# A decoder step on one core: the sampled tokens' attention handed out in 27 small steps between the prompt's steps, in place of nine large ones

## The chip, the cores and the metric

The kernel runs on one core of a Trainium2 chip. The metric is the device time of one launch in microseconds (us). A core has five engines that run their own instruction queues in order: TensorE (PE in the profile, with its weight loads as PEld), VectorE (DVE), ScalarE (ACT), GpSimd (POOL) and SyncE (SP), which here only issues DMA transfers.

## The reference, cut to what matters

One decoder layer. 1024 prompt tokens and 8 x 8 sampled tokens (8 sequences, 8 new tokens each) go through the same weights. Each token's normalised input is projected to three head groups: a gated short convolution, a dilated sliding-window attention of 6 heads (B), and a sliding-window attention with sinks of 6 query and 2 key heads (C). Their outputs go through one output projection; then comes a second norm and a SwiGLU feed-forward network.

```python
def apply_layer(x, mod, mixer, g_mix, g_ffn, w_out, w_gate_up, w_down):
    shift1, scale1, gate1, shift2, scale2, gate2 = mod
    mix, states = mixer(rmsnorm(x, g_mix) * (1 + scale1) + shift1)
    x = x + gate1 * (mix @ w_out)
    x = x + gate2 * swiglu(rmsnorm(x, g_ffn) * (1 + scale2) + shift2, w_gate_up, w_down)
```

The sampled tokens attend over a cache of past keys and values in HBM (2048 positions for B, 128 for C, for each of 8 sequences) and over their own 8 new tokens: scores, a masked softmax, and the weighted sum of values. The prompt tokens need nothing of the cache.

## The kernel before, in words

Activations lie transposed, 128 channels by 1088 tokens. The tokens are cut into three column groups, 0 to 365, 366 to 731 (both prompt only) and 732 to 1087, whose last 64 columns are the sampled tokens. A product in full precision is done as three matmuls per block of 128 rows (`mm3`, L204 to L206: high by high, high by low, low by high); a weight half (256 KB) is loaded by SP (`load`, L97, five buffers `wraw`) and split into a high and a low part on ScalarE (L90) and VectorE (L91; four buffers `wsp`).

After the prompt's attention two things are open: the sampled tokens' attention, and, for the first two column groups, everything that follows. Two generators hold them:

- `sample_steps` first does the three C head pairs, each with 2 x 128 cached positions, then the three B head pairs (p = 0, 1, 2). For a B pair: key loads of 512 KB (`stream_in`, L658 and L660, seven buffers `raw`), scores on TensorE (`scores`, L667) in three segments of 512, 512 and 264 columns, a running minimum on VectorE after each (`mins`, L671; scores are negated), then in `probs` one exponential over the whole row (L680), transposes (L690) and their copies (L691), then in `weigh` the products with the values (L701) for the two halves `par` of the sequences, each over 10 value blocks and the new tokens (`vn`), a scaled copy (L704), two transposes (L707) and copies into `mixS` (L712). Each B pair loads 10 key and 10 value tiles.
- `ahead_steps` holds the first two column groups' further way, 24 steps: two that split the attention output (`split_mix`), eight of the output projection (`w_out`, 48 matmuls each, with L768 to add the result), one for the root mean squares (`rstd`: squares L798, sums L799, L802; root L233 to L239, with the square root on ScalarE at L234; broadcast L806), one for the second norm (`second_norm`: L823 on VectorE, L825 on ScalarE, L826 on VectorE, eight blocks for each column group), four of gate and up (`gate_up`, 96 matmuls each, followed by a modulation tile, `late_mod`, whose loads `wmod` use the same `wraw` buffers and whose products are L179), and eight of the down projection (24 matmuls each).

The loop before gives two steps of `ahead_steps` after every step of `sample_steps`; the rest follows. Then the third column group, which holds the sampled tokens, is split into `mx` (L619 to L624), which needs all of `mixS`, and goes through the output projection.

The code's order is not the last word: the framework that builds the kernel puts each engine's instructions into an order by a timeline of its own, within what the data and the buffers allow. The queues on the chip are then fixed.

## Time and profile before

| what | value |
|---|---|
| median of 3 runs | 1393.7 us (1387.84 to 1393.89) |
| the profiled execution's own time | 1396.23 us |
| its span | 1394.2 us |
| TensorE busy | 1345.8 us (97%) |
| VectorE, ScalarE, GpSimd busy | 850.7, 596.0, 199.1 us |
| DMA | 190.90 MB, mean 137 GB/s |

The profile is of one execution. Its busy time of TensorE counts overlapping matmuls as busy, so the places where the engine stands are read from the timelines, not from the share. Times in the rows are us from the start of the span.

### The profile page before, as it was taken

How to read it: one execution, taken by the hardware profiler on the slowest of the kernel's cores; microseconds unless marked ns; L12 is line 12 of the kernel's file. 1: busy time of each engine (PE TensorE's matmuls, PEld its weight loads, DVE VectorE, ACT ScalarE, POOL GpSimd, SP SyncE). 2: the span in 40 equal slices, each digit the busy share in tenths (PEclk: the TensorE clock that was granted, in tenths of full speed). 3: DMA queues.
4: the chain of work that ended last, by engine and by line, in shares of the span. 5: the costliest groups of instructions: out<-in, count | busy, mean ns of one | idle time of the engine just before them, and what ended most of it. 6: DMA issues, size and time to landing. Idle time of an engine off the chain costs nothing.

```text
span 1394.2 us, 23856 instructions
## 1 busy us (share of the span) xinstructions
PE 1345.8 (97%) x9097; PEld 1281.3 (92%) x9097; DVE 850.7 (61%) x2016; ACT 596.0 (43%) x1227; POOL 199.1 (14%) x283
## 2 busy tenths in 40 slices
PE   7999999999999997999999999999999999999994
PEld 5889999988898886888999999999999999999994
DVE  4558868356676436325669766666666656566666
ACT  5488875466765324232345323232322222222252
POOL 2042310211101000000010111111111111111114
PEclk9999999999999998999999999999999999999996
DMA  9343431353406669775444413141423232323103
GB/s 362 111 154 100 144 100 32 122 183 107 145 24 228 225 237 333 249 297 182 115 136 123 128 61 91 57 155 61 153 90 129 88 125 91 122 92 121 52 23 129
DMA packets 77187, 190.90 MB, mean 137 GB/s; under 512 B 14048, under 2 KB 23808, under 8 KB 76288
## 3 DMA queue, kind: packets, MB, share of 16 engines
q1 hardware_dynamic: 73376, 135.67, 29.8%
q10 hardware_dynamic: 3536, 53.65, 10.7%
q8 instruction: 72, 1.18, 0.3%
q14 instruction: 43, 0.35, 0.1%
q0 software_dynamic: 160, 0.04, 0.0%
HBM read 181.32 MB, written 59.33 MB: 173 GB/s over the span
## 4 chain that ended last, share of the span: by engine, by line
PE 88%; DMA 4%; DVE 3%; ACT 2%; issue 2%; POOL 1%; SPq 0%; POOLq 0%; ACTq 0%; DVEq 0%
PE ps_g L204 20%; PE ps_g L206 19%; PE ps_g L205 19%; PE ps_s L205 3%; PE ps_s L204 3%; PE ps_s L206 3%; PE ps_o L582 3%; PE ps_t L204 2%; PE ps_t L205 2%; PE ps_t L206 2%; PE ps_t L573 2%; DMA wraw<-in_w_gu 2%; PE ps_s L529 1%; PE ps_s L530 1%; PE ps_g L179 1%
## 5 line engine op out<-in xcount | busy, mean ns | idle before, releaser
L204 PE MATMUL ps_g<-act,wsp 128*128 128x366 f32 (+1 forms) x1192 | 396.5, 334 | 2.2 <-DVE u L327 0.9
L205 PE MATMUL ps_g<-act,wsp 128*128 128x366 f32 (+1 forms) x1192 | 396.0, 332 | 0.0
L206 PE MATMUL ps_g<-act,wsp 128*128 128x366 f32 (+1 forms) x1192 | 392.9, 332 | 0.5 <-DVE wsp L91 0.3
L90 ACT ACTIVATE wsp<-wraw 128x512 fp32r<-128x512 f32 x232 | 145.8, 630 | 273.0 <-PE ps_g L206 174.9
L91 DVE TENSOR_TENSOR wsp<-wraw,wsp 128x512 fp32r<-128x512 f32 x232 | 167.2, 722 | 151.1 <-ACT wsp L90 145.5
L204 PEld LDWEIGHTS ps_g<-act,wsp 128*128 128x128 f32 x1192 | 225.3, 189 | 9.9 <-issue 3.3
L205 PEld LDWEIGHTS ps_g<-act,wsp 128*128 128x128 f32 x1192 | 225.7, 189 | 4.2 <-issue 2.3
L206 PEld LDWEIGHTS ps_g<-act,wsp 128*128 128x128 f32 x1192 | 224.7, 189 | 4.7 <-issue 3.1
L204 PE MATMUL ps_g<-hid,wsp 128*128 128x366 f32 (+3 forms) x464 | 153.6, 333 | 4.6 <-DVE ts L772 3.3
L205 PE MATMUL ps_g<-hid,wsp 128*128 128x366 f32 (+3 forms) x464 | 152.8, 329 | 1.5 <-DVE hid L857 1.4
L206 PE MATMUL ps_g<-hid,wsp 128*128 128x366 f32 (+3 forms) x464 | 153.1, 330 | 0.0
L204 PEld LDWEIGHTS ps_g<-hid,wsp 128*128 128x128 f32 x464 | 88.2, 190 | 7.8 <-DVE cv L768 3.8
L90 ACT ACTIVATE wsp<-tw 128x512 fp32r<-128x512 f32 x64 | 40.5, 633 | 122.2 <-PE ps_g L206 59.0
L205 PEld LDWEIGHTS ps_g<-hid,wsp 128*128 128x128 f32 x464 | 88.4, 191 | 2.3 <-DVE hid L857 2.1
L205 PE MATMUL ps_s<-act,wsp 128*128 128x366 f32 x272 | 90.2, 332 | 0.0
L204 PE MATMUL ps_s<-act,wsp 128*128 128x366 f32 x272 | 90.2, 331 | 0.0
L206 PE MATMUL ps_s<-act,wsp 128*128 128x366 f32 x272 | 90.0, 331 | 0.0
L206 PEld LDWEIGHTS ps_g<-hid,wsp 128*128 128x128 f32 x464 | 88.4, 190 | 0.0
L768 DVE SCALAR_TENSOR_TENSOR p_q<-ps_g,MOD,p_q 128x366 f32<-128x366 f32 (+3 forms) x99 | 55.4, 570 | 42.3 <-PE ps_g L206 42.2
L768 DVE SCALAR_TENSOR_TENSOR p_qc<-ps_g,MOD,p_qc 128x366 f32<-128x366 f32 (+3 forms) x99 | 56.5, 572 | 39.4 <-PE ps_g L206 37.6
L976 POOL TENSOR_TENSOR tw<-wraw 128x512 f32<-128x512 f32 x16 | 21.3, 1334 | 347.2 <-DMA wraw<-in_w_gu 209.5
L543 ACT ACTIVATE Sb<-Sb,st 128x257 f32<-128x257 f32 (+5 forms) x96 | 60.5, 632 | 21.1 <-DVE st L535 20.3
(337 smaller groups left out, 2319.3 us busy)
## 6 DMA issues: line engine op xcount, KB each, us to landing
wraw<-in_w_gu SPq DMA_DIRECT2D x112, 256.0 KB, 2.7
wraw<-in_wmod SPq DMA_DIRECT2D x64, 256.0 KB, 3.7
raw<-in_bk SPq DMA_DIRECT2D x30, 512.0 KB, 7.5
raw<-in_bv SPq DMA_DIRECT2D x30, 512.0 KB, 8.0
wraw<-in_w_in SPq DMA_DIRECT2D x36, 256.0 KB, 4.8
wraw<-in_w_d SPq DMA_DIRECT2D x36, 256.0 KB, 2.6
mraw<-in_wmod SPq DMA_DIRECT2D x32, 256.0 KB, 5.2
wraw<-in_w_out SPq DMA_DIRECT2D x32, 256.0 KB, 2.7
```

Of the source, the lines that this page charges most:

```text
L90: S.activation(sp[:, 0, :], raw, AF.Copy)
L91: (V if not state["sub"] or state["n"] % state["sub"] else G).tensor_tensor(sp[:, 1, :], raw, sp[:, 0, :].bitcast(F32), op=OP.subtract)
L179: ins = PE.matmul(ps[32 * q:32 * q + 32, :256], lhsT=csil[:, 4 * hf + q, :], rhs=raws[2 * hf + q // 2][:, q % 2 * 256:q % 2 * 256 + 256], ...
L204: PE.matmul(ps[:, :n], lhsT=w_hi, rhs=a(0, ak), start=first and j == 0, stop=False, **kw)
L205: PE.matmul(ps[:, :n], lhsT=w_hi, rhs=a(1, ak), start=False, stop=False, **kw)
L206: PE.matmul(ps[:, :n], lhsT=w_lo, rhs=a(0, ak), start=False, stop=last and j == m - 1, **kw)
L529: PE.matmul(ps[:, :sn], lhsT=QH[:, qsl], rhs=KS[hd][:, kk], start=True, stop=False)
L543: S.activation(Sb[:, :ne], Sb[:, :ne], AF.Exp, scale=-1.0, bias=m, accum_out=st[:, 3:4])
L573: PE.transpose(pt[:, col:col + 128], Sb[:, (kb - k0) * 128:(kb - k0 + 1) * 128], ident)
L582: PE.matmul(po[:, q0:q0 + w], lhsT=Vt[:, kb, hd].rearrange("p a b -> p (a b)"), rhs=PT[:, hl, c0:c0 + w], start=fresh, stop=ch is chunks[- ...
L768: ins = V.scalar_tensor_tensor(x1[m][:, c0:c0 + k], ps[:, :k], MOD[:, gate + m, 0:1], x1[m][:, c0:c0 + k], op0=OP.mult, op1=OP.add)
L976: G.tensor_tensor(t1, b12, b11, op=OP.subtract)
```

## The change

`sample_steps` gives control back more often: after each of the three score segments of a B pair (not only after the whole of them), after `probs` as before, and inside `weigh` after value blocks 4 and 10 of the first half and block 4 of the second (`nt` is 10 for B). That makes 3 + 3 x 8 = 27 steps in place of 3 + 3 x 2 = 9. The loop then gives one step of `ahead_steps` after each of them but every fifth, after which it gives none: 22 steps in all where it gave 18, so that two down steps are left at the end, not six. No operation's operands change.

```diff
+PACE = (1, 1, 1, 1, 0)
...
@@ weigh @@
                     PE.matmul(po[32 * j:32 * j + 32, par * 128:par * 128 + 128], lhsT=PT[:, k, 32 * j:32 * j + 32],
                               rhs=vn[:, new, :] if vt is None else vt[:, j, :], start=(k == 0), stop=(k == nt))
+                if nt > 1 and k in (4, nt) and par + k < nt + 1:
+                    yield
...
@@ sample_steps @@
-            weigh(PT, st, lambda par, k: vc[par][:, :, :128], 1, 0, 5 + j)
+            yield from weigh(PT, st, lambda par, k: vc[par][:, :, :128], 1, 0, 5 + j)
...
                 mins(ps, n, Sb[:, sl], maskS[:, sl], st[:, seg - 1:seg] if seg else 3.0e38, st[:, seg:seg + 1])
+                yield
             PT = probs(Sb, 1280, st, st[:, 2:3])
             yield
...
-            weigh(PT, st, values, 10, 1 + p, 2 + p)
+            yield from weigh(PT, st, values, 10, 1 + p, 2 + p)
             yield
...
     ahead = ahead_steps()
-    for _ in sample_steps():
-        for _ in range(2):
+    for i, _ in enumerate(sample_steps()):
+        for _ in range(PACE[i % len(PACE)]):
             next(ahead, None)
     for _ in ahead:
         pass
```

What this does to the queues is seen in the order of the built programs. The line numbers of the changed kernel are two to five higher (L667 is L669, L680 is L682, L690 is L692, L701 is L703, L802 is L807, L806 is L811, L825 is L830, L97 is L99). An `x16` there counts instructions; the profile records each of these full-precision products, other than transposes, as two.

TensorE before, between the last matmul of the output projection and the first of the gate (head pair p = 1):

```order
L667 MATMUL ps_s<-raw,Q 32x256 x28
L802 MATMUL ps_g<-ones,free 128x1 x3
L667 MATMUL ps_s<-raw,Q 32x256 x4
L667 MATMUL ps_s<-raw,Q 32x264 x4
L806 MATMUL ps_g<-ident,ir_y 128x128 x3
L802 MATMUL ps_g<-ones,free 128x1 x3
L667 MATMUL ps_s<-raw,Q 32x264 x4
L690 MATMUL ps_t<-ident,SM 128x128 x10
L701 MATMUL ps_o<-raw,PTs 32x128 x18
L690 MATMUL ps_t<-ident,px 128x128
L701 MATMUL ps_o<-raw,PTs 32x128 x4
L806 MATMUL ps_g<-ident,ir_y 128x128 x3
```

TensorE in the changed kernel, at the same place:

```order
L669 MATMUL ps_s<-raw,Q 32x256 x16
L807 MATMUL ps_g<-ones,free 128x1 x3
L669 MATMUL ps_s<-raw,Q 32x264 x8
L811 MATMUL ps_g<-ident,ir_y 128x128 x3
L807 MATMUL ps_g<-ones,free 128x1 x3
L692 MATMUL ps_t<-ident,SM 128x128 x10
L703 MATMUL ps_o<-raw,PTs 32x128 x32
L692 MATMUL ps_t<-ident,px 128x128
L703 MATMUL ps_o<-raw,PTs 32x128 x8
L703 MATMUL ps_o<-vn,PTs 32x128 x4
L703 MATMUL ps_o<-raw,PTs 32x128 x32
L811 MATMUL ps_g<-ident,ir_y 128x128 x3
```

Sixteen score products (the first segment) have moved ahead of this place, before the last 48 matmuls of the output projection; 44 value products stand between the last of the transposes and the second broadcast where 4 did. Behind the last row 24 gate matmuls of the first column group follow; before, ten more L701, 4 gate matmuls and 56 L701 did.

ScalarE before, at the same place (L234 is the square root, L680 the exponential of p = 1, L825 the second norm):

```order
L234 ACT_TABLE_LOAD
L234 ACTIVATE ir_y<-ir_v 128x3
L825 ACTIVATE act<-free,MOD 128x366 x8
L234 ACTIVATE ir_y<-ir_v 128x3
L680 ACT_TABLE_LOAD
L680 ACTIVATE SM,stb<-SM,stb 128x1288
L691 ACTIVATE PTs<-ps_t 128x512 x2
L691 ACTIVATE PTs<-ps_t 128x384
L825 ACTIVATE act<-free,MOD 128x366 x8
```

ScalarE in the changed kernel:

```order
L236 ACT_TABLE_LOAD
L236 ACTIVATE ir_y<-ir_v 128x3
L682 ACT_TABLE_LOAD
L682 ACTIVATE SM,stb<-SM,stb 128x1288
L830 ACTIVATE act<-free,MOD 128x366
L693 ACTIVATE PTs<-ps_t 128x512
L830 ACTIVATE act<-free,MOD 128x366
L693 ACTIVATE PTs<-ps_t 128x512
L830 ACTIVATE act<-free,MOD 128x366 x6
L236 ACT_TABLE_LOAD
L236 ACTIVATE ir_y<-ir_v 128x3
L693 ACTIVATE PTs<-ps_t 128x384
```

The exponential has moved ahead of the eight L825, and a second load of the root's table stands behind them.

SP's queue in the changed kernel from the last modulation loads of the gate stage on, with the last key and value loads of p = 2 between the down and output weights (before, one value load stood behind five of the down weights, two behind six, and all the others earlier):

```order
L99 DMA wraw<-in_wmod 128x512 x4
L99 DMA wraw<-in_w_dn 128x512 x6
L662 DMA raw<-in_bk 128x4x256 x2
L660 DMA raw<-in_bv 128x1024 x4
L99 DMA wraw<-in_w_dn 128x512
L660 DMA raw<-in_bv 128x1024
L99 DMA wraw<-in_w_dn 128x512
L99 DMA wraw<-in_w_out 128x512
L660 DMA raw<-in_bv 128x1024 x2
L99 DMA wraw<-in_w_out 128x512 x3
L660 DMA raw<-in_bv 128x1024 x3
L99 DMA wraw<-in_w_out 128x512 x2
```

All ten value loads and the last two key loads of p = 2 now stand in the down stage's part of the queue. On TensorE 24 matmuls stand between the scores of the first two segments and those of the third there, and 50 between the last L707 and the first matmul of the third column group, where 167 did.

## Rows read from the trace of the kernel before

**Rows 1.** The page: the granted clock in 40 slices of the span (part 2), and the shares by engine of the chain that ended last (part 4).

```profile
PEclk9999999999999998999999999999999999999996
...
PE 88%; DMA 4%; DVE 3%; ACT 2%; issue 2%; POOL 1%; SPq 0%; POOLq 0%; ACTq 0%; DVEq 0%
```

**Rows 2.** Busy time of each engine in two stretches of 20 us (columns: stretch, its length; then TensorE, its weight loads, VectorE, ScalarE and GpSimd, each as busy us and instructions; granted clock, busy share of the DMA engines, GB/s).

```profile
520.00:540.00 20.00, 12.30 (x147) 8.08 (x139) 13.01 (x38) 10.55 (x18) 1.62 (x6) 0.74 0.79 283
640.00:660.00 20.00, 20.00 (x122) 19.97 (x121) 13.38 (x36) 6.92 (x21) 0.12 (x1) 1.00 0.46 140
```

**Rows 3.** Timeline of TensorE from 518 to 548 us (columns: start us, length us, engine, line, operation, tiles, shape, count; in brackets the idle time before and what ended it).

```profile
519.15 3.23 PE L667 MATMUL ps_s<-raw,Q 128*32 128x256 f32 x56
...
525.93 0.94 PE L806 MATMUL ps_g<-ident,ir_y 128*128 128x128 f32 x6
...
534.59 2.49 PE L690 MATMUL ps_t<-ident,SM 128*128 128x128 f32 x10 [5.92 <-ACT SM L680]
537.01 1.78 PE L701 MATMUL ps_o<-raw,PTs 128*32 128x128 f32 x36
...
539.34 0.94 PE L806 MATMUL ps_g<-ident,ir_y 128*128 128x128 f32 x6
...
540.99 0.43 PE L204 MATMUL ps_g<-act,wsp 128*128 128x366 f32 x1
...
542.52 1.93 PE L701 MATMUL ps_o<-raw,PTs 128*32 128x128 f32 x64
545.97 0.64 PE L701 MATMUL ps_o<-raw,PTs 128*32 128x128 f32 x16 [1.52 <-DMA raw<-in_bv]
...
546.76 0.43 PE L205 MATMUL ps_g<-act,wsp 128*128 128x366 f32 x1
```

**Rows 4.** Timeline of ScalarE in the same stretch.

```profile
520.42 1.28 ACT L234 ACT_TABLE_LOAD   x1
...
527.53 4.14 ACT L825 ACTIVATE act<-free,MOD 128x366 fp32r<-128x366 f32 x8 [3.96 <-DVE free L823]
...
531.78 1.28 ACT L680 ACT_TABLE_LOAD   x1
533.08 1.37 ACT L680 ACTIVATE SM<-SM,stb 128x1288 f32<-128x1288 f32 x1
...
535.74 0.60 ACT L691 ACTIVATE PTs<-ps_t 128x512 f32<-128x512 f32 x1 [1.20 <-PE ps_t L690]
...
539.09 0.49 ACT L691 ACTIVATE PTs<-ps_t 128x384 f32<-128x384 f32 x1 [1.90 <-PE ps_t L690]
```

**Rows 5.** Timeline of VectorE in the same stretch.

```profile
520.58 0.55 DVE L799 TENSOR_TENSOR free<-free 128x366 f32<-128x366 f32 x1
521.15 0.69 DVE L671 CUSTOM_DVE_ANT_0 SM<-ps_s,maskS 128x512 f32<-128x512 f32 x1
...
526.90 1.10 DVE L823 SCALAR_TENSOR_TENSOR free<-cv,MOD,ps_g 128x366 f32<-128x366 f32 x2 [1.03 <-PE ps_g L806]
...
529.44 1.60 DVE L823 SCALAR_TENSOR_TENSOR free<-p_qc,MOD,ps_g 128x366 f32<-128x366 f32 x3
...
531.44 4.16 DVE L826 SCALAR_TENSOR_TENSOR act<-free,MOD,act 128x366 fp32r<-128x366 f32 x8
535.52 0.16 DVE L235 RECIPROCAL ir_y<-ir_y 128x3 f32<-128x3 f32 x1
```

**Rows 6.** Four stretches of 3 us around the same place (columns as in rows 2).

```profile
524.00:527.00 3.00, 2.06 (x26) 1.26 (x18) 1.43 (x7) 0.00 (x0) 0.41 (x2) 1.00 1.08 369
530.00:533.00 3.00, 0.00 (x0) 0.00 (x0) 3.00 (x10) 2.98 (x6) 0.00 (x0) 0.50 1.01 414
536.00:539.00 3.00, 3.00 (x44) 2.01 (x43) 0.46 (x3) 0.94 (x2) 0.00 (x0) 0.65 0.02 8
539.00:542.00 3.00, 3.00 (x47) 2.25 (x50) 1.69 (x4) 1.54 (x4) 0.00 (x0) 1.00 0.86 261
```

**Rows 7.** Elsewhere on TensorE: a piece of the chain that ended last (start us, us, what), and four rows of the timeline, three of which end a wait.

```profile
490.07 0.87 PE ps_t L690 x8
...
500.33 0.65 PE L701 MATMUL ps_o<-raw,PTs 128*32 128x128 f32 x16 [1.28 <-DMA raw<-in_bv]
...
609.25 0.43 PE L204 MATMUL ps_g<-act,wsp 128*128 128x366 f32 x1 [0.26 <-ACT wsp L90]
...
625.14 1.07 PE L179 MATMUL ps_g<-wraw,csil 128*32 128x256 f32 x16
...
633.26 0.65 PE L701 MATMUL ps_o<-raw,PTs 128*32 128x128 f32 x16 [1.74 <-DMA raw<-in_bv]
```

**Rows 8.** Loads: a key load on the chain that ended last (start us, us from issue to landing), a value load in the timeline of SP's queue (columns as in rows 3), and the value loads issued from 520 to 560 us (count, KB each, median us from issue to landing).

```profile
519.85 3.84 DMA raw<-in_bk
...
628.01 0.42 SPq L658 DMA_DIRECT2D raw<-in_bv  x1
...
raw<-in_bv SPq DMA_DIRECT2D x10, 512.0 KB, 7.7
```

**Rows 9.** The end of the sampled tokens' work: its last transposes on TensorE, the last operand of the third column group on VectorE (both from the timelines), and the matmuls that read `mx` (count, shortest, median and longest ns, first and last start).

```profile
642.06 0.38 PE L707 MATMUL ps_t<-ident,ob 128*128 128x128 f32 x2
...
649.16 0.21 DVE L624 TENSOR_TENSOR mx<-mixS,mx 128x64 fp32r<-128x64 f32 x1
...
L204 PE MATMUL ps_g<-mx,wsp x64: 320/325/329, 666.9 to 697.7; 128*128 128x356 f32 x64
```

## The prediction

> **What bounds the kernel now.** I read the page first. TensorE carries 88% of the chain that ended last, at full clock nearly everywhere; the one visible dent lies a third of the way through [rows 1]. The table of 20 us stretches puts the dent at 520 to 540 us: TensorE busy 12.3 of 20 us at 0.74 of its clock. Of the time after the sampled tokens' work, 640 to 660 is full and holds 122 matmuls [rows 2], so the pitch is 20 / 122 = 0.164 us; I use 0.167 for the 366 columns here. The kernel is thus a TensorE queue, and an edit that adds or removes no arithmetic can only gain or lose where that queue waits. The timelines of TensorE, ScalarE and VectorE around the dent show why it waits.
>
> The other tokens' last output-projection matmul ends at 519.15 and the first gate matmul starts at 540.99; steady work returns at 546.76 [rows 3]. Between them lies the second norm: square root, broadcast (L806), scaling (L823), rounding (L825, L826), for two column groups. Only the sampled tokens' work can fill it. It doesn't: the transposes L690 wait 5.92 us [rows 3] for an exponential that stands on ScalarE behind eight L825 (527.53 to 531.67) and a table load [rows 4]. Because the second broadcast stands behind those transposes and the products behind them, it comes at 539.34 [rows 3], though its reciprocal root was on VectorE at 535.52 [rows 5]. Meanwhile the granted clock fell from 1.00 to 0.50, that is from 2.4 to 1.2 GHz [rows 6], after TensorE had worked with gaps since 521; it was back only after some 3 us of renewed work.
>
> Prices at full clock: L667, each recorded as two passes, 28 of them in 3.23 us = 0.115; L701, 32 in 1.93 = 0.060 [rows 3]; L690 0.87 / 8 = 0.109 [rows 7]. At half clock L701 took 1.78 / 18 = 0.099 and L690 0.249 [rows 3]. From 519.15 to 546.76 the kernel does 40 L667 (4.6), 12 small L802 and L806 (1.8 by their 0.9 per six passes), 11 L690 (1.2), 88 L701 (5.3) and 4 matmuls (0.7): 13.6 us of work in 27.6, so **14 us are lost in this one place**. Elsewhere in the stage TensorE's visible waits are 1.28 us at 500.33 and 1.74 at 633.26 for value loads, and 0.26 at 609.25 for a weight [rows 7].
>
> **The dent after the change.** No arithmetic is added; what moves is order. The head pair whose work falls in the dent is the same, but its first 16 L667 now come before the last projection, and the exponential stands on ScalarE ahead of the L825 (both in the order shown with the change). I follow the new order with the old durations, from the same 519.15.
>
> - 16 L667 end at 521.0. VectorE is free at 521.13 [rows 5], takes the minimum L671 (0.7), then the first root; ScalarE's table is already loaded at 521.70 [rows 4]. With a second, shorter L671 (at most the same) between the small steps, the first broadcast comes at about 524.0 instead of 525.93. L823 then runs 524.9 to 529.0 instead of 526.90 to 531.04 [rows 5].
> - The exponential: table load 1.28, then 1.37 plus its read [rows 4], from 523.65 to 525.2, where it was 533.08 to 534.5. The first eight transposes and their copies of 0.6 are done at 527.7 (two copies with one L825 between). Products can start there, 9.3 us before 537.01 [rows 3].
> - ScalarE then owes the rest of the L825 until 530.8, a reload of the root's table that is new (1.28), the second root and the last copy of 0.49 [rows 4]: 532.8.
> - TensorE's order puts 44 L701 after that copy and the second broadcast behind them. At 0.060 they end at 535.5, at 0.099 at 537.2. VectorE has the second root at 534.7, after eight L826 that start at 529.5 (4.16) [rows 5], so L701 decides.
> - After the broadcast stand 24 matmuls of the first column group (4.0 us), which hide the second group's norm: broadcast to L823 0.98, L823 4.1, the first L826 0.52 [rows 5], so its first operand is there 5.6 us later, at 541.1 or 542.9. There steady work resumes.
>
> Against 546.76 the changed kernel has then 20 more matmuls behind it (+3.3 us), 11 L701 still ahead (-0.65), and had 16 L667 moved ahead of 519.15 (-1.85). Gain = 546.76 + 0.8 - (541.1 to 542.9) = **6.5 to 4.7 us**. I take 5.0: the new order leaves gaps of the same kind from 522 on, so I expect the clock to fall again at much the same moment. The one load that could bind here is the second half's values: seven buffers, three of them refilled only when the first products have run (about 528.4). At a landing of 7.7 us [rows 8] the second of them comes at 536.6, where TensorE wants it at 535.1 at full clock, 536.5 at half: 1.5 us late or not at all. With 3.84 [rows 8] it is hidden, and I count nothing.
>
> One rule speaks against this part. ScalarE's timeline has the next activation 1.30 us after the start of a table load of 1.28 [rows 4], so a switch costs the load and no more. The Trainium skill, page "ScalarE: Activation LUTs", section "What ACT_TABLE_LOAD costs", gives about 1283 ns for the load and some 1380 ns for a drain beside it, 2.66 us for every switch. The trace agrees on the load and shows no drain at this place. By the page the two switches on the new chain (to the exponential, and back to the root) would cost 1.4 us more each, and the 5.0 would be 2.2.
>
> **The other waits.** The second half's value loads of the first head pair now have more work in front of them: by the new order 48 matmuls, 8 us, stand after the first half of its products, where the second half's followed directly; I count the 1.28 us [rows 7] as gone. But its scores move some 47 matmuls (7.8 us) ahead, while key buffers come free as before. The nearest row: a key load landed 3.84 us after its issue [rows 8]. From the L667 that frees a buffer to the one that needs its refill lie 12 + 4 L667, 4 matmuls and 16 L701 = 3.5 us. That is a new wait of 0.3 by that row, 2 under load; I take **+0.8**, between them and nearer the row, since few loads are in flight there.
>
> The third head pair moves from the gate stage to the down-projection stage. The 1.74 us at 633.26 and the 0.26 at 609.25 go, because the gate stage keeps only eight key loads, sent early. In their place: the last two key loads stand in SP's queue behind six down weights, whose buffers are freed only by the last modulation product (L179). In the kernel before, a value load stood in the same position and was issued at 628.01, 2.9 us after L179's 625.14 [rows 7, 8], and was used at 633.26, 8.1 us after it. In the new order TensorE arrives at the first of the two after L179 (1.1), 27 L667 (3.1) and 24 matmuls (4.0) = 8.2 us, and at the second 0.6 later, which lands about 1.3 later still (512 KB at the 414 GB/s of 530 to 533 [rows 6]): about 1 us of wait. Three value loads stand behind the fourth output weight, whose buffer needs the third down step's matmuls; I make that 0 to 2.5 us, 0.5 taken, because its issue (some 20 us after L179) precedes its use by about 5 us, what the 628.01 load took. Together **+1.5**, from 0 to 3.5.
>
> At the stage's end only two down steps are left as cover, not six. In the kernel before, the last transposes (642.06) were followed 7.3 us later by the last operand of the third column group (649.37), needed from 666.7 on [rows 9]. In the new order 50 matmuls, 8.3 us, stand between: just enough, since TensorE takes that operand last. Cost nothing; without cover, the 7.3.
>
> Sum: -5.0 - 1.3 - 1.7 - 0.3 + 0.8 + 1.5 = **-6.0 us**. The profiled execution took 1396.2 us, 2.0 beside its span of 1394.2, and stands 0.18% over the median of 1393.7; by its own time the sum gives 1390.2. I take the same 6 us from the median: **1388**. Bounds: best -6.5 - 3.3 = -9.8, 1384; worst with all waits at their upper end, -4.7 - 3.3 + 2 + 3.5 = -2.5, 1391.
>
> **Rivals.**
> 1. The order helps less than drawn: values land late in the dent, the second norm starts no earlier for it, and new waits on loads eat the small gains. For: the loads share 16 engines that were busy at 1.0 and over at 524 and at 530. Against: they stood at 0.02 from 536 to 539 [rows 6], so TensorE and not the transfers was late. Gain 0 to 2.5: 1391 to 1394.
> 2. The clock stays up, and no new wait arises: 1384.
> 3. A table switch between activations in flight costs about twice its row, 2.6 us, since ScalarE must first run empty: two switches on the chain, +2.6, so -3.4 and 1390. The 1.30 us row speaks against it. The skill's section named above is this rule.
> 4. Slower: SP's queue. Value loads stand behind output weights that wait for down steps, and TensorE in order stands at the value products. If each refill costs its whole landing of 7.7 us on TensorE (two groups of loads, 15.4) the sum is -8.3 + 15.4 = +7: 1401. It decides once the new waits exceed 8.3 us. Against: the loads' issue precedes use by some 5 us.
>
> **Numbers.** Likeliest case 0.48 (1385 to 1391); rival 1 0.24; 2 0.12; 3 0.07; 4 and other losses 0.09. The range that leaves out 2 in 10 is 1382 to 1395. About 0.5% (7 us) is what a measurement can tell here; faster than 1386.7 are rival 2 and the lower part of the likeliest, 0.37; slower than 1400.7 0.07; the same 0.56.
>
> **What would show it.** The exponential before the L825 and ending some 6 us after the last projection; the second broadcast 16 to 18 us after it, not 20; TensorE steady 22 to 24 us after it, not 27.6; no wait for L680 over 2 us; waits of about 1 us for the last keys after the last modulation product. Wrong if TensorE waits over 3 us for values in the down stage, if the clock stays low past the second broadcast, or if the third column group's first matmul waits for its operand.

## The result, and the profile of the changed kernel

The changed kernel took 1381.45 us (median of 6 runs, 1379.34 to 1385.72), the kernel before 1393.80 beside it: a ratio of 0.9923, 95% interval 0.9904 to 0.9941. A second set of runs gave 0.9922 (0.9902 to 0.9942). So it is 0.8% faster, 11 to 12 us. Its median is half a microsecond under the lower end of the predicted range (1382 to 1395); by the ratio, from the 1393.7 that the prediction started from, it is 1383.0, just inside. It falls in the class "faster by over 0.5%", to which the prediction gave 0.37, not in the likeliest.

The profiled execution took 1385.72 us, its span 1383.8, 10.4 us less than before. Its page, the granted clock in 40 slices and the chain's shares (part 2 and 4, as in [rows 1]):

```profile
PEclk9999999999999999999999999999999999999997
...
PE 87%; DVE 4%; DMA 4%; ACT 3%; issue 2%; POOL 1%; SPq 0%; POOLq 0%; ACTq 0%; DVEq 0%
```

The dent in the clock line is gone, though not the dent itself, as the stretches show (columns as in rows 2):

```profile
480.00:500.00 20.00, 20.00 (x250) 18.90 (x253) 7.48 (x13) 6.09 (x11) 0.00 (x0) 1.00 0.71 238
500.00:520.00 20.00, 20.00 (x174) 18.12 (x170) 7.39 (x17) 4.43 (x8) 0.80 (x2) 1.00 0.84 287
520.00:540.00 20.00, 15.59 (x237) 12.64 (x230) 13.88 (x39) 12.31 (x22) 0.86 (x4) 0.83 0.95 342
...
560.00:580.00 20.00, 18.00 (x116) 16.99 (x116) 4.66 (x11) 4.50 (x8) 0.00 (x0) 0.98 0.62 211
...
620.00:640.00 20.00, 20.00 (x169) 18.09 (x171) 7.27 (x17) 6.28 (x10) 0.00 (x0) 1.00 0.92 342
640.00:660.00 20.00, 20.00 (x232) 19.34 (x225) 11.44 (x32) 6.70 (x21) 0.12 (x1) 1.00 0.43 133
```

From 520 to 540 TensorE is now busy 15.6 us with 237 instructions at 0.83, where it was 12.3 us with 147 at 0.74 [rows 2]. The waits for values at 500 are gone. From 560 to 580, where TensorE was busy for all 20 us before, there is a new hole of 2 us.

TensorE around the dent (timeline, as [rows 3]):

```profile
519.26 1.93 PE L669 MATMUL ps_s<-raw,Q 128*32 128x256 f32 x32
...
523.93 0.93 PE L811 MATMUL ps_g<-ident,ir_y 128*128 128x128 f32 x6 [0.94 <-DVE ir_y L241]
...
532.48 1.08 PE L703 MATMUL ps_o<-raw,PTs 128*32 128x128 f32 x16 [2.79 <-ACT PTs L693]
...
533.76 3.64 PE L703 MATMUL ps_o<-raw,PTs 128*32 128x128 f32 x64
537.33 1.30 PE L811 MATMUL ps_g<-ident,ir_y 128*128 128x128 f32 x6
...
542.91 0.43 PE L206 MATMUL ps_g<-act,wsp 128*128 128x366 f32 x1
```

and ScalarE (as [rows 4]):

```profile
522.41 1.28 ACT L682 ACT_TABLE_LOAD   x1
523.71 1.37 ACT L682 ACTIVATE SM<-SM,stb 128x1288 f32<-128x1288 f32 x1
...
530.55 1.28 ACT L236 ACT_TABLE_LOAD   x1
531.84 0.20 ACT L236 ACTIVATE ir_y<-ir_v 128x3 f32<-128x3 f32 x1
531.95 0.47 ACT L693 ACTIVATE PTs<-ps_t 128x384 f32<-128x384 f32 x1
```

The 5.92 us wait for the exponential has gone; what is left is 2.79 us for the last copy, behind the reload of the root's table, and 3.64 us for 32 products at half clock (granted clock 0.50 from 533 to 537).

**Where the 10.4 us lie.** The start records of the same three matmuls, found in every trace, cut the span in four. The first cut is some 6 us ahead of the sampled tokens' first score product, the second is the first matmul of the third column group, the third some 50 us before the end. All in us:

| profile | start to 1st cut | sampled stage | middle | last stage |
|---|---|---|---|---|
| before | 440.0 | 226.9 | 675.5 | 51.8 |
| before, second profile | 440.3 | 231.6 | 673.7 | 49.2 |
| changed | 439.8 | 220.6 | 675.0 | 48.5 |
| changed, second profile | 437.2 | 225.8 | 674.2 | 47.2 |

In the first pair the sampled stage gives 6.3 us, the last stage 3.4, the rest 0.8. The prediction had 6.0 for the stage and nothing elsewhere. One profile of each is little, as the second ones show: the sampled stage of one kernel differs by 5 us between its two profiles. Hence the experiments.

### The profile page after: what moved, and what is told of

Its sections match the earlier page's. It is cut to its first block, busy times and chain, and to the rows that moved or that the text cites. A ratio compares the mean times of both kernels' runs of the same rounds, so it can differ in the third digit from the quotient of the medians.

```text
span 1383.8 us, 23859 instructions
## 1 busy us (share of the span) xinstructions
PE 1340.4 (97%) x9097; PEld 1279.6 (92%) x9097; DVE 851.8 (62%) x2016; ACT 597.0 (43%) x1228; POOL 200.0 (14%) x283
## 4 chain that ended last, share of the span: by engine, by line
PE 87%; DVE 4%; DMA 4%; ACT 3%; issue 2%; POOL 1%; SPq 0%; POOLq 0%; ACTq 0%; DVEq 0%
PE ps_g L206 19%; PE ps_g L207 19%; PE ps_g L208 19%; PE ps_s L207 3%; PE ps_s L206 3%; PE ps_s L208 3%; PE ps_t L206 2%; PE ps_t L207 2%; PE ps_t L208 2%; PE ps_o L584 2%; PE ps_t L575 2%; PE ps_o L703 1%; PE ps_s L531 1%; DMA wraw<-in_w_in 1%; PE ps_s L669 1%
```

## The experiments

Ratios are to the kernel before, timed beside each other, with 95% intervals. The dent is the stretch of rows 3, from the last matmul of the output projection to steady work in the gate stage; the gate stage is the four gate and up steps behind it, the down stage the down steps up to the third column group. Four theories are tested:

- Theory 1: the dent's length follows from the order of the queues there, and that is the gain.
- Theory 2: a part of the gain comes from VectorE's order in the last stage.
- Theory 3: work lying between the gate steps covers their waits for weights.
- Theory 4: the third head pair costs in the gate stage through its loads, which hold up the weights.

**Both kernels once more.** No edit.

> The changed kernel once more, unaltered, for a second profile. Theory 1 (the dent, the stretch from the last output-projection matmul to steady work in the gate stage): it is a matter of queue order, so the dent lasts 24 us again, as in the first profile of the changed kernel (27.6 in the kernel before), and the time is 0.991 to 0.994 of the kernel before. Theory 2 (the tail): a part of the gain, some 3 us, lies in the last 30 us of the span, because the static order of VectorE is other there; then the granted clock comes back to full in the last stage again and the last stage is as short as in the first profile. Rival to theory 2: the clock there is chance; then the last stage may as well show 0.50 to the end, as the profile of the kernel before did, and be some 3 us longer, with nothing else altered.

> The kernel before once more, unaltered, for a second profile. Counted against full-speed prices, its first profile lost 13.4 us in the dent, 4 in the rest of the gate stage, 2.8 in the down stage, and the last stage ran at half clock from 1368 us to the end. Theory 1 (queue order makes the dent): 12 to 14 us lost in the dent again, with the same 5.9 us wait for the exponential. On the last stage: if the clock is chance there, it may come back to full for some us this time, as it did in both profiles of the changed kernel; if the order of VectorE decides, it is at half clock to the end again.

Measured: 0.9922 (0.9902 to 0.9942) for the changed kernel; of the kernel before this is a second profile. Its transposes waited again for the exponential (timeline of TensorE, second profile of the kernel before):

```profile
534.87 2.49 PE L690 MATMUL ps_t<-ident,SM 128*128 128x128 f32 x10 [5.60 <-ACT SM L680]
```

and in the changed kernel the clock did not fall in the dent this time; but its gate stage had larger holes (stretches of its second profile):

```profile
520.00:540.00 20.00, 15.05 (x251) 12.42 (x242) 16.08 (x42) 14.61 (x25) 0.86 (x4) 1.00 1.01 389
560.00:580.00 20.00, 18.14 (x119) 17.13 (x118) 5.58 (x14) 4.54 (x9) 0.00 (x0) 1.00 0.64 219
580.00:600.00 20.00, 17.36 (x115) 16.26 (x114) 5.11 (x10) 4.55 (x9) 0.00 (x0) 1.00 0.58 199
600.00:620.00 20.00, 16.93 (x141) 14.14 (x139) 5.44 (x12) 4.43 (x9) 0.42 (x2) 0.94 0.60 205
```

So the dent's wait belongs to the queues, as it came in both profiles of the one kernel and in neither of the other; whether the clock falls beside it, and how long the gate stage waits, varies from run to run. In the last stage the clock did come back to full in the second profile of the kernel before, for some 6 us.

**Parts of the change.** Score yields alone, 18 small steps:

```diff
-PACE = (1, 1, 1, 1, 0)
+PACE = (1,)
-                if nt > 1 and k in (4, nt) and par + k < nt + 1:
+                if False:
                     yield
```

> Only the yields after each score segment are kept, those within the value products are dropped; 18 small steps, one step of the other tokens' work after each, so 18 of those as before. In its queues the exponential of the second head pair stands ahead of the square root, with the transposes and all 88 value products in the dent, and no second load of the root's table. Theory 1 (only what stands in the dent counts): first broadcast some 5.8 us after the last projection, second at 13 to 14, steady work at 19 to 21 instead of 24; so 3 to 5 us faster than the changed kernel, 0.988 to 0.991 of the kernel before. Rival (the gain is that of the fineness, or of the pace of 22 steps, through fewer waits for loads all over the stage): it loses the weigh yields and the pace, so it is no faster than the changed kernel, 0.994 to 1.000.

All small steps, 18 steps of the other tokens' work:

```diff
-PACE = (1, 1, 1, 1, 0)
+PACE = (1, 1, 0)
```

> All 27 small steps are kept, but only 18 steps of the other tokens' work are given between them, two of three, as many as before. In its queues the dent holds no exponential at all: transposes, 92 value products and 20 score products of the third pair. Theory 1: first broadcast about 4.2 us after the last projection, second at 12 to 14, steady work at 18 to 20; 4 to 6 us faster than the changed kernel, 0.987 to 0.990 of the kernel before. Rival (the pace of 22 steps, which moves the third head pair into the down stage and removes the waits for its values, is what gained): the waits for values of 1.7 us in the gate stage return and the time is that of the changed kernel or up to 3 us more, 0.993 to 0.996.

Nine large steps, 22 steps of the other tokens' work (both kinds of yield out):

```diff
-PACE = (1, 1, 1, 1, 0)
+PACE = (2, 2, 3, 2, 3, 2, 3, 2, 3)
```

> The nine large steps of the kernel before are kept, but 22 steps of the other tokens' work are given between them as in the changed kernel. In its queues the dent holds 40 score products and no exponential, transposes or value products; both broadcasts stand close together. Theory 1, by the same rows: first broadcast at 5.5 to 7 us after the last projection, steady work at about 21, 6 us earlier than before, but 99 products and transposes (6.5 us) are left for later and 20 more gate matmuls (3.3 us) are done: 3 us faster than the kernel before, 0.997 to 0.999, and some 5 us slower than the changed kernel in that stage. Rival (the pace gained): as fast as the changed kernel, 0.991 to 0.994. Its last stage has nearly the order of the kernel before on VectorE: if that order costs the clock, its last 30 us are some 3 us longer than in the changed kernel; if the clock there is chance, either.

Measured: 1.0040 (1.0026 to 1.0055), 0.9979 (0.9962 to 0.9995) and 1.0004 (0.9985 to 1.0022). None is near what theory 1 gave the first two (0.987 to 0.991); the third is at or just above the range it gave. In its strict form, that the dent's queue alone counts, theory 1 falls. Why the second gains so little isn't shown: its profile's sampled stage took 223.2 us, close to the changed kernel's. The first kernel shows why its dent is no shorter (timeline of TensorE, score yields alone):

```profile
522.89 1.47 PE L693 MATMUL ps_t<-ident,SM 128*128 128x128 f32 x8 [1.61 <-ACT SM L683]
...
534.44 0.64 PE L704 MATMUL ps_o<-raw,PTs 128*32 128x128 f32 x16 [2.69 <-DMA raw<-in_bv]
536.20 0.64 PE L704 MATMUL ps_o<-raw,PTs 128*32 128x128 f32 x16 [1.11 <-DMA raw<-in_bv]
...
538.24 1.08 PE L670 MATMUL ps_s<-raw,Q 128*32 128x256 f32 x8 [1.18 <-DMA raw<-in_bk]
...
541.79 1.65 PE L812 MATMUL ps_g<-ident,ir_y 128*128 128x128 f32 x6
```

With 88 products and the next keys in the dent, TensorE gets to the sampled tokens' data before they have landed and waits three times, 5.0 us in all: the second broadcast comes at 541.8, not at the 532 to 533 that theory 1 had (13 to 14 us after the last projection at 519). Here more work in the dent helps only as far as its loads keep up.

**The exponential put back.** The changed kernel, with one order edge on ScalarE:

```diff
+            if g == 0 and k == KC - 1:
+                hold.append(ins)
...
-        S.activation(Sb[:, :ne], Sb[:, :ne], AF.Exp, scale=-1.0, bias=m, accum_out=st[:, 3:4])
+        with behind():
+            S.activation(Sb[:, :ne], Sb[:, :ne], AF.Exp, scale=-1.0, bias=m, accum_out=st[:, 3:4])
```

`ins` is the eighth L830 of the first column group, and `behind` puts the next exponential, that of the second B pair, after what `hold` has.

> The changed kernel with one edge added on ScalarE: the exponential of the second head pair stands behind the eight roundings of the first column group, where the kernel before has it. The pace, the 27 steps and the last stage are those of the changed kernel. In its queue TensorE has 22 value products between the transposes and the second broadcast, not 76. Theory 1 (the exponential's place in ScalarE's queue fills the dent): the transposes wait some 5 to 6 us for it again, and 54 products (3.2 us) are left for the gate stage: 2 to 4 us slower than the changed kernel, 0.994 to 0.996 of the kernel before. Rival (the gain of the changed kernel lies elsewhere: the last stage, fewer waits for loads): the same time as the changed kernel, 0.991 to 0.993.

Measured: 1.0013 (0.9993 to 1.0033), median 1393.96. The whole gain is gone, 12 us, three times the most that was expected. TensorE and ScalarE:

```profile
533.33 2.69 PE L699 MATMUL ps_t<-ident,SM 128*128 128x128 f32 x10 [7.08 <-ACT SM L689]
...
539.17 0.93 PE L818 MATMUL ps_g<-ident,ir_y 128*128 128x128 f32 x6
```

```profile
526.36 4.14 ACT L837 ACTIVATE act<-free,MOD 128x366 fp32r<-128x366 f32 x8 [3.14 <-DVE free L835]
...
531.82 1.37 ACT L689 ACTIVATE SM<-SM,stb 128x1288 f32<-128x1288 f32 x1
```

The wait is 7.08 us, and the second broadcast comes 19.1 us after the last projection (520.09), not 18.1, with 54 products fewer before it (3.2 us): some 4 us of the 12 in the dent. Its profile's sampled stage took 229.9 us, 8 more than the mean of the changed kernel's queues (below), so some 4 more fell in the gate stage, into which those products moved. The last 4 are a matter of what is compared: the changed kernel's two profiled executions took 1385.7 and 1386.3 us, 4 to 5 over their medians, and this one (1394.18) took its median. Profile against profile the difference is 8 us, and 7 to 8 of them lie in the sampled stage.

**Only the third head pair put back.** Same queue up to the second norm, then another table of steps:

```diff
-PACE = (1, 1, 1, 1, 0)
+PACE = (1, 1, 1, 1, 0, 1, 1, 1, 1, 0, 1, 1, 1, 1, 0, 1, 0, 0, 1, 0, 0, 1, 0, 1, 0, 1, 1)
```

> The changed kernel with another table of steps: as it up to the second norm, and then 13 small steps over four gate steps and two down steps, so that the third head pair stands in the gate stage, as in the kernel before, and six down steps are left at the end. The dent's queue and the last stage are as in the changed kernel. Theory 3 (the gate stage of the changed kernel waits for gate weights and modulation tiles, 2 to 9 us in its two profiles, because the third pair's work no longer lies between them): these waits go and only the waits for values of up to 2 us come back; 1 to 4 us faster than the changed kernel, 0.989 to 0.992 of the kernel before. Rival (the pair's loads cost in the gate stage as much as its work covers, as predicted before: 2.0 us of waits there): the same as the changed kernel or up to 2 us slower, 0.992 to 0.994.

Measured: 0.9969 (0.9948 to 0.9991), median 1387.96: 6 us slower than the changed kernel, against both expectations. Theory 3, that work lying between gate steps covers the waits for weights, falls. The chain that ended last shows what stands there instead (this kernel, pieces: start, us, what):

```profile
605.20 0.62 PE ps_o L704 x16
605.83 0.33 SPq L661
606.25 0.38 SPq L100
606.74 4.70 DMA wraw<-in_w_dn
...
612.91 9.41 DMA wraw<-in_w_dn
622.40 0.64 ACT wsp L93
...
625.19 0.28 ACT modev L187
625.51 1.02 PE ps_g L189 x4
```

A value load (L661) waits on SP for a buffer that the products free; the weight load (L100) stands behind it; two weight loads later the modulation product waits for ScalarE, which waits for the weight. TensorE waits twice for a modulation tile here (its timeline):

```profile
578.23 0.61 PE L189 MATMUL ps_g<-sel,modev 128*128 128x9 f32 x4 [2.93 <-ACT modev L187]
...
625.51 1.02 PE L189 MATMUL ps_g<-sel,modev 128*128 128x9 f32 x4 [3.65 <-ACT modev L187]
```

**Theory 4**: the pair costs in the gate stage through its loads, which stand in SP's queue ahead of the weights and share the transfer engines with them. The chain has a second reading, which no run tests: its longest piece, 9.41 us, is a weight load issued at 612.91, just behind two cache copies (transfers that pass cached keys on to an output) that ScalarE's queue issued (timeline of ScalarE):

```profile
611.57 0.52 ACTq L110 DMA_DIRECT2D out_bk_a<-in_bk  x1
612.13 0.60 ACTq L110 DMA_DIRECT2D out_bk_b<-in_bk  x1
```

**The loads taken out.** Nine of the third pair's ten value loads left out, so that its products read one tile again and again and its output is wrong; with the pair in the gate stage (twice) and in the changed kernel:

```diff
+                if p == 2:
+                    held[par, k // 2] = held.get((0, 0))
-                if (par, k // 2) not in held:
+                if held.get((par, k // 2)) is None:
```

> The kernel with the third head pair in the gate stage (gate_cover), which was 6 us slower than the changed kernel with the same dent, once more, with nine of the third pair's ten value loads left out: its products read one tile again and again, so the sampled tokens' output of that pair is not computed. TensorE's queue is the same but for a few places. Theory 4 (the third pair costs in the gate stage not by its work but by its 512 KB loads, which delay the gate and modulation weights that TensorE then waits for): 4 to 7 us faster than with the loads, 0.990 to 0.993 of the kernel before, and waits for modulation tiles of 3 to 4 us gone. Rival (the place of the work itself costs, or the weights' own ring of buffers does): 0.996 to 0.998, as with the loads.

> The kernel with the third pair in the gate stage and nine of its value loads left out, once more, unaltered (that pair's output is not computed), since its interval of 0.9903 to 0.9959 still touches that of the same kernel with the loads, 0.9948 to 0.9991. Theory 4 (the loads cost in the gate stage): 0.991 to 0.995 again, so 2 us or more under the kernel with the loads. Rival (the first timing was low by chance): 0.996 to 0.998. In the gate stage of its profile, theory 4 has one wait of some 3 us for a modulation tile at most, as in its first profile, where the kernel with the loads had two of 3.3 and 3.9 us.

> The control for the run before: the changed kernel with the same nine value loads of the third pair left out (so that pair's output is not computed either); there they lie in the down stage. Theory 4 as worked in the prediction (the down stage has room for these loads; waits of 0 to 3.5 us were expected there, 1.3 and 3.1 us were lost in two profiles, of all causes): 0 to 2 us faster than the changed kernel, 0.991 to 0.993. Rival (the loads cost wherever they stand): 4 us or more faster, under 0.990.

Measured: 0.9931 (0.9903 to 0.9959) and 0.9943 (0.9920 to 0.9966) with the pair in the gate stage, so 5.3 and 3.6 us come back by the ratios, with TensorE's queue nearly the same; 0.9951 (0.9927 to 0.9974) in the changed kernel, where leaving the same loads out gains nothing. The sampled stage took 227.1 us in the profile with the loads, 221.0 and 222.1 in those without; but the changed kernel's own took 220.6 and 225.8, so profiles alone don't decide it. The landing of the gate weights in the gate stage (DMA issues: count, KB, median us to landing) was, with the loads,

```profile
raw<-in_bv SPq DMA_DIRECT2D x9, 512.0 KB, 7.4
...
wraw<-in_w_gu SPq DMA_DIRECT2D x11, 256.0 KB, 4.4
```

without them

```profile
wraw<-in_w_gu SPq DMA_DIRECT2D x11, 256.0 KB, 3.9
```

and in the changed kernel, whose gate stage has two key loads and no value load,

```profile
wraw<-in_w_gu SPq DMA_DIRECT2D x11, 256.0 KB, 3.2
```

This landing alone shows little: it is 3.5 in the second profile without the loads, and 3.0 in the kernel before, which has seven value loads in the same stage. Theory 4 holds in its sign; its size rests on ratios whose intervals overlap with that of the kernel with the loads. Of the two waits for modulation tiles (2.93 and 3.65 us) the runs without loads kept the first (3.10 and 2.88), and the second time a part of the other (1.38), so the loads are not their only cause.

**The last stage.** The sums of squares of the last column group put behind the last two down products, on VectorE alone (`last` keeps the results named there; one more edge, not shown here, holds an add of block 5 back):

```diff
+AFTER_ADD = {2: ("mul", 6), 3: ("add", 6), 4: ("add", 7)}
...
+    def behind_tail(n, k):
+        return tc.issue_after(last[AFTER_ADD[k]].ins) if n == 256 and k in AFTER_ADD else ExitStack()
...
-            eng(adds[k]).tensor_add(acc[:, :n], acc[:, :n], sq[:, :n])
+            with behind_tail(n, k):
+                eng(adds[k]).tensor_add(acc[:, :n], acc[:, :n], sq[:, :n])
```

> The changed kernel with the last stage's order on VectorE put back near that of the kernel before: the sums of squares of the last column group stand behind the last two down products' results again, as there; no other engine's queue is altered. The stretch from 1342 us of the kernel before to the end took 51.8 and 49.2 us in its two profiles (51.5 in the nine-step kernel, which has its order), 48.5 and 47.2 in those of the changed kernel (47.8 to 49.5 in the five others with its order). Theory 2 (VectorE's order in the last stage is worth 2 to 3 us): 2 to 3 us slower than the changed kernel, 0.994 to 0.996 of the kernel before. Rival (the clock there falls and comes back by chance, as the second profile of the kernel before showed): the same time as the changed kernel within 1 us, 0.991 to 0.993.

Measured: 0.9909 (0.9880 to 0.9939): not slower than the changed kernel. Theory 2 falls, for this order at least; the order is near that of the kernel before, not the same. Its sampled stage, a third profile of the changed kernel's queues there, took 220.0 us. The clock in the last stage (stretches: the kernel before, its second profile, the changed kernel):

```profile
1370.00:1380.00 10.00, 7.75 (x37) 7.46 (x36) 6.23 (x27) 4.30 (x12) 0.00 (x0) 0.50 0.08 28
```

```profile
1370.00:1380.00 10.00, 5.91 (x37) 5.74 (x38) 8.39 (x36) 4.74 (x12) 1.75 (x2) 0.83 0.42 154
```

```profile
1360.00:1370.00 10.00, 6.34 (x41) 6.10 (x41) 8.36 (x35) 4.73 (x12) 1.48 (x2) 0.83 0.38 142
```

The clock is 0.50 all through these 10 us in one profile of the kernel before and 0.83 in the other. By the start records, the way from the 151st of the last stage's 184 matmuls to the 181st took 14.4 us in the first and 11.8 in the second: nearly all of the 2.6 us between its two last stages (51.8 and 49.2).

**A redone dent.** Both groups' sums first, both roots, then the exponential:

```diff
-        r = [second_rstd(g) for g in range(2)]
+        ps2 = [square_sums(GRP[g], NADD, acc_tile(g)) for g in range(2)]
+        r = [bcast(ps2[g], GRP[g][1]) for g in range(2)]
+        hold.append(roots[-1])
```

`square_sums` is the first part of `rstd`, `bcast` its root and broadcast, and the exponential stands behind the second root.

> The changed kernel with the dent redone: both column groups' sums of squares, then both square roots one behind the other, then the exponential; so the table is not loaded back and the second broadcast does not stand behind value products. In its queue the sample transposes and products lie between the first gate matmuls. Theory 1: both broadcasts within 2 us of each other some 5 to 7 us after the last projection; VectorE then paces the dent with 16.6 us of scaling and rounding; first gate matmul at 8 to 10 us instead of 17 to 19 and the loss in the dent 4 to 6 us instead of 7 to 9: 2 to 5 us faster than the changed kernel, 0.988 to 0.991 of the kernel before. Rival (loads bound here: the value loads of this head pair and the keys of the next come no faster, or the gate weights do not): what the dent gains is waited for at loads, and the time is that of the changed kernel, 0.991 to 0.993.

Measured: 0.9922 (0.9894 to 0.9950), the changed kernel's own ratio. By the start records the first gate matmul came 10.5 us after the start of the output projection's last, not 19.4, but the 37th 27.6 us after it, as in the changed kernel's first profile (27.4). What paces the dent there isn't shown: VectorE is busy with the scaling and rounding of both groups to 540, and from 530 on TensorE has hardly a gap either. No version tried beats the changed kernel by more than its interval.

## Why the prediction was right or wrong, step by step

**The dent: right, nearly to the row.** Worked: first broadcast 524.0, exponential from 523.65, last copy done at 532.8, second broadcast when the 44 products end (535.5 to 537.2), first operand of the second group at 541.1 or 542.9. Traced: 523.93, 523.71, 532.4, 537.33, and its first matmul at 542.91. Measured as the prediction did it (the second group's first matmul against 546.76 + 0.8, from the same last projection), the dent gave 4.8 us in the first profile, where the clock fell for 6.8 us, and 6.7 in the second, where it did not fall; 4.7 to 6.5 was forecast and 5.0 taken. TensorE's order there is the same, 262 matmul records, in seven profiles (the changed kernel's two, the third pair put back, the three without loads, the last stage's order): the clock was at half for 6.8 us in five, for 3.4 in one and not at all in one. So the fall that was forecast is the rule, and rival 2's clock the exception. That the exponential's place makes the dent's wait is shown by putting it back: the wait is there again, and with it the whole gain goes, of which some 4 us lie in the dent. With the dent as changed and the third pair left in the gate stage the gain is 0.31%, 4.3 us, where the steps for the dent, the values at 500 and the early keys gave 5.5 (in that kernel the waits for modulation tiles stand against them). Two readings are off without touching the sum: 12 small L802 and L806 are 24 passes, so 3.6 us by the price given and not 1.8, and some 12 us, not 14, were lost in the dent; and TensorE was busy to 522.4 (519.15 + 3.23 [rows 3]), so its gaps did not begin at 521.

**The table switch: the row was the price.** The exponential starts 1.30 us after its table load starts, the root 1.29 us after its reload, with no drain. By the Trainium skill, page "ScalarE: Activation LUTs", section "What ACT_TABLE_LOAD costs", each switch would have cost 2.66 us; the trace does not show it, and rival 3 falls with it.

**The values at 500.33: right.** Both stretches from 480 to 520 are full. **The early keys: right in kind.** The changed kernel's timeline has

```profile
465.47 0.64 PE L669 MATMUL ps_s<-raw,Q 128*32 128x256 f32 x8 [0.34 <-DMA raw<-in_bk]
```

0.34 us in this row, inside the 0.3 to 2 given; 0.8 was taken.

**The third head pair: the step that failed.** It was priced as waits for the pair's own loads: -1.7 and -0.3 in the gate stage, +1.5 in the down stage, so -0.5. The move is worth about 6 us beside the new dent (0.9969 against 0.9922), by a term that was put at half a microsecond. The down stage took the loads for nothing: TensorE is busy without a hole from 620 to 660, and leaving nine loads out gains nothing there. What the step didn't see is what those loads do to others: taking them out of the gate stage gives back 4 to 5 of the 6 us, if the two ratios are taken as they stand. Rival 4 had the right queue and the wrong victim: it feared values behind weights, and the cost, as far as the loads make it, was weights behind values, in the stage they left. Why the kernel before had no such waits for modulation tiles, with the pair in the same stage but in large steps, isn't settled. In its SP queue seven of the pair's value loads stand in one block, in the other kernel they lie in several places among the weights; and the table below has another difference.

**A cost that no step had: the gate stage now waits for weights.** Where the pair's work went, TensorE arrives at the gate weights early. In the changed kernel (first profile)

```profile
577.79 0.44 PE L206 MATMUL ps_g<-act,wsp 128*128 128x366 f32 x1 [2.00 <-DVE u_ff L846]
```

VectorE's name is put there because it came last; ScalarE had just split a weight (575.94) after 8.94 us of waiting for its load. In the second profile the chain runs through nothing but weights for 60 us:

```profile
603.61 9.38 DMA wraw<-in_w_dn
613.07 0.64 ACT wsp L92
...
614.46 2.70 DMA wraw<-in_w_dn
...
617.79 0.37 ACT modev L186
618.21 1.02 PE ps_g L188 x4
```

It cost 2.0 us of holes in one profile and 7.6 in the other (60 less the busy time of the three stretches from 560 to 620). The records of all 14 kept profiles show where slow loads stand. From 540 to 616 a weight load that was issued less than 1.4 us behind a cache copy took 7.4 us or more to land (7.4 to 9.4 in 16 loads with a landing on record); of the other 257, four in five took 2.5 to 5. How many fell just behind a copy goes with TensorE's waits for weights and modulation tiles:

| profile | weight loads just behind a copy | TensorE's waits for them, us |
|---|---|---|
| before, both profiles | 0, 0 | 0.3, 0.6 |
| changed, both profiles | 1, 3 | 2.0, 7.6 |
| third pair in the gate stage | 3 | 6.6 |
| the same without loads, both profiles | 1, 1 | 3.1, 4.3 |
| changed, without loads | 1 | 2.0 |

In the six other profiles one or two such loads stand with 1.4 to 6.4 us of these waits. So the value loads may cost what they cost by moving weight loads into the copies' way. That is argued: no run here moves the copies. And a slow load costs only where TensorE has nothing else: in the kernel before one weight load took 13.4 us to land, and TensorE waited 0.26 us for it [rows 7]. In sum, over the profiles, the sampled stage gained 7.1 us (mean of two profiles before, 229.2; of three with the changed queues, 222.1), close to the 6.0; but the sum came out by a term for the third pair that was too small and a missing one for the weights that stands against it. That is luck.

**The last stage: missing, and partly open.** The sum had nothing there; the first two profiles have 3.4 us, the means of all (two before, three with the changed queues up to there, 50.5 and 48.2) 2.3. Clock and no more is what the second profile of the kernel before and the order experiment say. But over the timed runs the mean granted clock was 0.9869 before (84 runs) and 0.9895 after (12): about 36 and 29 us of each span at 1.2 GHz, if the rest is at 2.4. Part of that is the dent (10 us before, 7 or none after). Why the last stage should come back to full clock more often after the change isn't settled: the three profiles with the order before, or one close to it in the nine-step kernel, took 51.8, 49.2 and 51.5, the others 47.2 to 49.5, and an order exactly as before in the changed kernel was not tried.

**The cover at the stage's end: right.** No wait there, with 50 matmuls between the last transposes and the third column group; before, the trace has 147 of them there, not the 167 given with the change.

## What to carry to other kernels

When a stage is moved, price it by what its transfers do to the others in the queue and on the engines, not only by its own waits: here 9 loads of 512 KB cost some 4 to 5 us beside a stream of weights and nothing where there was room. A long operation on an in-order engine belongs ahead of the work that has slack: putting one exponential back behind eight roundings cost the whole gain. And filling a gap with more work helps only as far as that work's loads and the engine that sets the gap's length allow.

## What was not expected of the hardware

- A 256 KB weight load landed 2.70 us after its issue in one place and 9.38 us in another of the same stage; the slow one was issued at 603.61, within 0.5 us of two cache copies on ScalarE's queue (603.12 and 603.68). The 16 weight loads of all profiles from 540 to 616 that were issued less than 1.4 us behind a copy took 7.4 to 9.4 us. The transfer engines' mean busy share was 0.99 and 1.10 from 603 to 609 and 0.11 from 609 to 612, so only few of them still worked when it landed at 613.0. The Trainium skill, page "DMA: Bandwidth & Descriptors", section "Queues, rings and completion order", has each engine take turns between the queues that have work for it; the slow load beside the copies agrees with that.
- With the same program and the same queues, TensorE's granted clock fell to half in the dent for 6.8 us in one profile and not at all in another, beside the same waits (0.94 and 2.79 us in the first, 0.93 and 2.79 in the second).
